# A hybrid decoder layer: the up projection as one level of Strassen's product, the gates beside the cached-key attention

## The chip, the core and the metric

The kernel is one launch on one core of a Trainium2 chip. Its engines work side by side and wait for each other by semaphores: TensorE (PE; its weight loads are listed as PEld), VectorE (DVE), ScalarE (ACT), GpSimd (POOL) and SyncE (SP), which only issues DMAs. Matmul operands stand in SBUF, matmul results in PSUM. The metric is the device time of one execution in microseconds, as a median of several runs; the profile shows one execution.

## The reference

One inference step of one decoder layer for 1024 prompt tokens and 8 sequences of 4 new tokens (32 "sample" tokens) which attend to 1024 cached tokens each, stored as 8 pages of 128. All in float32; model width 1024, FFN width 2816.

```python
proj = x @ w_in                      # q | k | v | hgrn q, f, i, g | gate_a | gate_b
oa = diff_attention(rope(q), rope(k) (+ cached pages), v)      # 4 heads, two score maps each
ob = hgrn2_scan(...)                                           # 4 heads, chunkwise
merged = sigmoid(gate_a) * (oa @ w_branch_a) + sigmoid(gate_b) * (ob @ w_branch_b)
h = layer_norm(ALPHA * x + merged @ w_out)
a, g = split(h @ w_up, 2)            # 1024 -> 2 x 2816
c = conv_b + sum(ap[:, j:j + T] * conv_w[j] for j in range(3))  # causal, over tokens
y = (gelu(c) * g) @ w_down
out = layer_norm(ALPHA * h + y)
```

Outputs are `out` for both token sets, the new keys and values, the HGRN states and the last two rows before the convolution.

## The kernel before

**Arithmetic.** A float32 product runs on TensorE as three products of a reduced type: each operand is split into a high part (ACT copies it, line 130) and a low part (DVE subtracts the high part from the value, line 131), and `mm3` (lines 225 to 227) or `mm3s` (lines 235 to 237) add high x high, low x high and high x low. A weight tile of 128x512 therefore costs one ACT cast and one DVE subtraction, from `raw`, which SP loads, into `wh` and `wl`. Activations lie transposed, features in partitions and tokens in columns.

**Stages.** (1) Input projections and the four HGRN heads. (2) Attention of the prompt: `attn(h, ...)` for four heads, eight query blocks each. A block `i` with n = 128 (i + 1) keys makes two score maps on PE (lines 634, 635; the tile `scp`, of which the pool `ps_sc` has two), masks and reduces them to row maxima on DVE (lines 638, 641, 643), takes the exponentials on ACT (line 646), combines the maps on DVE (lines 648 to 650), transposes the result on PE (line 207), copies it back on ACT (line 203), and multiplies by the values on PE (line 662). (3) Gates: `proj_gate` makes 128 columns of gate_a or gate_b for all 1056 tokens (72 matmuls of 384 and 288 columns, a tanh on ACT, line 830, and a write to the DRAM tile `gsc`, line 831). There are 16 of them, and `do_gates(n)` does the next n: 2 stand behind the HGRN heads, 3 behind `attn(0)`, 2 behind `attn(1)`, 5 behind `attn(3)` and 4 behind the first `load_o`. A scheduler lays out the order of each engine, so that a gate's matmuls stand between those of an attention that is written before it. (4) For each half of the tokens (512, and 512 with the 32 sample tokens): `merge` (gated branches, line 946 to 948; output projection; LayerNorm; `turn_`, which transposes back and splits h into the SBUF tiles `hh` and `hl`), then `ffn`.

**ffn, one half.** For each m of 22 the columns m of `a` and of `g` are two products over the eight 128-row pieces of h, with token columns in two groups (256 and 256 in the first half, one of 512 there for m of 16 and more; 256 and 288 in the second). The convolution is three DVE operations (lines 1052 to 1054), Gelu is on ACT (line 1065), the product with g on DVE (line 1071), and a split leaves u in SBUF. `down` multiplies the 22 tiles of u by `w_down`, `rows` adds ALPHA h (POOL, line 1090) and the product (DVE, line 1091), turns the result, and `ln2` normalises it (POOL, lines 1138 and 1139).

**The sample attention.** `SampleAttn` gathers cached pages with indirect DMAs that POOL issues (line 723) into a tile `pg` of two buffers; `keys(b)` transposes them on DVE (line 743) and makes the scores on PE (line 749); `values(b)` multiplies by the gathered values (line 800). In this kernel `beside` spreads the 8 calls of `keys` and the 8 of `values` over the 22 steps m of the first half's up projection. Two half passes follow each other: merge, up, down, merge, up, down.

## Time and profile before

| | |
|---|---|
| median of 3 runs | 1805.58 us (1803.87 to 1806.1) |
| the profiled execution | 1803.07 us |
| its span in the trace | 1801.3 us |
| TensorE busy | 1761.8 us, 98% |
| VectorE busy | 1035.4 us, 57% |
| ScalarE busy | 747.9 us, 42% |
| GpSimd busy | 200.0 us, 11% |

From the trace the stages lie at these times: projections and HGRN to about 315 us, attention with its gates to about 735, first merge to about 840, up of the first half with the sample attention to 1145, down to 1262, second merge to 1388, up to 1655, down to 1790. Matmuls are pipelined, so that a matmul's shown duration (280 ns for 256 columns) is longer than the distance from its start to the next start (118 ns); the distance is what a further matmul costs. For the same reason a busy share near one doesn't exclude short waits on TensorE.

### The profile page before, as it was taken

The page shows a single profiled execution, that of the slowest core. Times are in us where ns is not written, and L with a number is a line of the kernel's source. Part 1 is how long each engine was busy: PE and PEld are TensorE (multiplying, and loading weights), DVE is VectorE, ACT ScalarE, POOL GpSimd, SP SyncE. Part 2 cuts the span into 40 slices and gives each one's busy share as a digit, 9 for nine tenths or more (in the row PEclk, how much of TensorE's full clock was granted, in tenths as well). Part 3 has the DMA queues.
Part 4 walks back from the last instruction along what each step waited for, and adds up shares of the span by engine and source line. Part 5 has one row for each costly group of instructions (what it writes and reads, how often), then busy time and mean ns, then how long its engine had stood idle before and what let it go on. Part 6 is the DMA issues. An engine that isn't in the chain of part 4 may idle for free.

```text
span 1801.3 us, 33741 instructions
## 1 busy us (share of the span) xinstructions
PE 1761.8 (98%) x13652; PEld 1654.1 (92%) x13652; DVE 1035.4 (57%) x2199; ACT 747.9 (42%) x1774; POOL 200.0 (11%) x280
## 2 busy tenths in 40 slices
PE   8999999999999999998999999999899999999996
PEld 8999999999999999887989987888888999999996
DVE  5757646765656653656776454444856655554336
ACT  6466354545553544425333433223325433443223
POOL 1000010120221010003030011000500000000013
PEclk9999999999999999998999999999999999999998
DMA  6110211212221222844556466424632332323234
GB/s 214 38 61 26 83 61 42 92 47 77 84 68 39 79 75 70 270 129 142 178 176 202 143 206 196 150 88 136 219 116 83 96 91 83 94 83 89 86 91 125
DMA packets 234832, 199.37 MB, mean 111 GB/s; under 512 B 8050, under 2 KB 213106, under 8 KB 230562
## 3 DMA queue, kind: packets, MB, share of 16 engines
q1 hardware_dynamic: 218432, 140.92, 26.0%
q0 software_dynamic: 9296, 47.44, 7.4%
q10 hardware_dynamic: 6948, 8.86, 1.5%
q8 instruction: 107, 1.75, 0.4%
q14 instruction: 49, 0.40, 0.1%
HBM read 173.00 MB, written 24.19 MB: 109 GB/s over the span
## 4 chain that ended last, share of the span: by engine, by line
PE 89%; DVE 4%; DMA 3%; ACT 2%; issue 1%; POOL 1%; SPq 0%; POOLq 0%; DVEq 0%; ACTq 0%
PE mm L236 14%; PE mm L235 14%; PE mm L237 14%; PE mm L225 11%; PE mm L227 10%; PE mm L226 10%; PE tp L207 3%; PE tp L662 2%; PE sb L405 2%; PE mm L246 1%; PE scp L635 1%; PE scp L634 1%; PE mx L225 1%; PE mx L227 1%; DMA c<-gsc 1%
## 5 line engine op out<-in xcount | busy, mean ns | idle before, releaser
L131 DVE TENSOR_TENSOR wl<-raw,wh 128x512 fp32r<-128x512 f32 (+1 forms) x404 | 286.3, 714 | 368.0 <-ACT wh L130 348.1
L130 ACT CAST wh<-raw 128x512 fp32r<-128x512 f32 (+1 forms) x404 | 244.9, 612 | 489.1 <-PE mm L236 371.2
L235 PE MATMUL mm<-hh,wh 128*128 128x256 f32 (+2 forms) x1312 | 386.9, 295 | 3.3 <-ACT hh L130 2.7
L236 PE MATMUL mm<-hl,wh 128*128 128x256 f32 (+2 forms) x1312 | 387.3, 295 | 1.4 <-DVE mv L910 1.4
L237 PE MATMUL mm<-hh,wl 128*128 128x256 f32 (+2 forms) x1312 | 387.3, 296 | 0.0
L235 PEld LDWEIGHTS mm<-hh,wh 128*128 128x128 f32 x1312 | 249.2, 190 | 13.7 <-issue 4.1
L236 PEld LDWEIGHTS mm<-hl,wh 128*128 128x128 f32 x1312 | 248.7, 190 | 6.9 <-DVE hl L131 2.1
L237 PEld LDWEIGHTS mm<-hh,wl 128*128 128x128 f32 x1312 | 248.6, 190 | 5.0 <-issue 0.6
L225 PE MATMUL mm<-xh,wh 128*128 128x384 f32 (+1 forms) x560 | 186.7, 334 | 0.8 <-ACT wh L130 0.8
L226 PE MATMUL mm<-xl,wh 128*128 128x384 f32 (+1 forms) x560 | 186.9, 334 | 0.0
L227 PE MATMUL mm<-xh,wl 128*128 128x384 f32 (+1 forms) x560 | 186.0, 332 | 0.0
L225 PE MATMUL mm<-wh,xh 128*128 128x256 f32 x480 | 136.5, 285 | 0.8 <-DVE rb L578 0.8
L226 PE MATMUL mm<-wl,xh 128*128 128x256 f32 x480 | 136.3, 284 | 0.2 <-DVE wl L131 0.2
L227 PE MATMUL mm<-wh,xl 128*128 128x256 f32 x480 | 135.9, 283 | 0.0
L225 PEld LDWEIGHTS mm<-xh,wh 128*128 128x128 f32 x560 | 105.3, 188 | 4.0 <-issue 2.3
L227 PEld LDWEIGHTS mm<-xh,wl 128*128 128x128 f32 x560 | 105.4, 188 | 1.8 <-issue 1.5
L226 PEld LDWEIGHTS mm<-xl,wh 128*128 128x128 f32 x560 | 105.4, 188 | 1.3 <-issue 0.8
L225 PEld LDWEIGHTS mm<-wh,xh 128*128 128x128 f32 x480 | 90.2, 188 | 1.5 <-issue 1.0
L226 PEld LDWEIGHTS mm<-wl,xh 128*128 128x128 f32 x480 | 90.4, 188 | 0.5 <-DVE wl L131 0.4
L227 PEld LDWEIGHTS mm<-wh,xl 128*128 128x128 f32 x480 | 90.5, 189 | 0.1
L203 ACT COPY s<-tp 128x512 f32<-128x512 f32 (+3 forms) x96 | 39.5, 426 | 101.2 <-PE tp L207 42.5
L1090 POOL TENSOR_TENSOR c<-hh,hl 128x512 f32<-128x512 f32 (+2 forms) x24 | 23.3, 970 | 476.1 <-DVE u20l L131 256.8
(670 smaller groups left out, 3772.6 us busy)
## 6 DMA issues: line engine op xcount, KB each, us to landing
raw<-in_w_up_dram SPq DMA_DIRECT2D x88, 512.0 KB, 3.8
raw<-in_w_in_dram SPq DMA_DIRECT2D x44, 512.0 KB, 3.8
raw<-in_w_down_dram SPq DMA_DIRECT2D x36, 512.0 KB, 3.6
raw<-in_w_out_dram SPq DMA_DIRECT2D x16, 512.0 KB, 3.7
raw<-in_w_down_dram SPq DMA_DIRECT2D x18, 384.0 KB, 3.1
gsc<-gt ACTq DMA_DIRECT2D x32, 192.0 KB, 1.9
raw<-in_w_branch_b_dram SPq DMA_DIRECT2D x16, 256.0 KB, 5.4
raw<-in_w_branch_a_dram SPq DMA_DIRECT2D x16, 256.0 KB, 3.6
```

Source lines behind the costliest of these rows:

```text
L130: S.copy(h, src)
L131: eng.tensor_tensor(l, src, h.bitcast(F32), ALU.subtract)
L203: S.copy(out, in_)
L207: PE.transpose(out, in_, ident[:n, :n])
L225: PE.matmul(ps, lhsT=ah, rhs=bh, start=(i == 0), stop=False)
L226: PE.matmul(ps, lhsT=ah, rhs=bl, start=False, stop=False)
L227: PE.matmul(ps, lhsT=al, rhs=bh, start=False, stop=(i == n - 1))
L235: PE.matmul(ps, lhsT=ah, rhs=bh, start=(k == 0), stop=False)
L236: PE.matmul(ps, lhsT=ah, rhs=bl, start=False, stop=False)
L237: PE.matmul(ps, lhsT=al, rhs=bh, start=False, stop=(k == n - 1))
L405: PE.matmul(p[:, a * 64:a * 64 + 64], lhsT=W[:, a * 128:a * 128 + 128], rhs=rhs[:, a * nb:a * nb + nb], start=True, stop=True)
L662: PE.matmul(po[:, :128], lhsT=aT[:, j * 128:(j + 1) * 128], rhs=v_[:, j], start=(j == 0), stop=(j == i))
```

## The change

The up projection is done once for all 1056 tokens, behind both merges, and by Strassen's scheme in the form with 15 additions: h^T is cut into two halves of the features and, for the prompt, two halves of the tokens (sample tokens 0 to 15 go with the first, 16 to 31 with the second), the weights into feature halves and into a and g. Seven products of half the depth take the place of eight. `operands` and `combine` make the seven operands from h (four additions on POOL in `combine`, splits on ACT and DVE), `wcombos(m)` makes the seven from the weights (four additions on POOL, seven splits), `product` is one of the seven for 256 or 272 columns, and the loop over m puts the results together (five additions on DVE, two on POOL, two copies on ACT, for each of two column chunks).

h goes to the DRAM tile `hT` and is read back for the second merge's `combine` and in `rows`, where it was an addition on POOL. The gated rows u go through the DRAM tile `uT`: their product with g is now on POOL, and `down_half` reads them and splits them. `down` is as before, apart from m = 0 and 1 of each half, which go together. The order is now merge, merge, up, down, down. The sample attention stands behind the prompt's attention, one call of `keys` or `values` (two, at two places) beside each of 14 gates; the other two gates stand behind the first `load_o`.

```diff
     hgrn(3, *lq, g, i23[1])
-    do_gates(2)
...
     attn(0, Q[0], K[0], v[0])
-    do_gates(3)
...
     v = proj_tok(1024, 1, vsl, vs_, O["v_p"], O["v_s"])
-    do_gates(2)
...
     attn(3, Q[1], K[1], v[1])
-    do_gates(5)
...
+    sample = SampleAttn(ap, av)
+    for i in range(14):
+        do_gates(1)
+        for b in range(8 * (i % 7) // 7, 8 * (i % 7 + 1) // 7):
+            (sample.keys if i < 7 else sample.values)(b)
...
+    def combine(c, cols, b11, b12, b21, b22, t3):
+
+        def put(o, x):
+            h, l = ops[c][o]
+            split(x, h[:, :, cols], l[:, :, cols])
+
+        put(B11, b11)
+        G.tensor_tensor(t3, b22, b12, ALU.subtract)
+        G.tensor_tensor(b12, b12, b11, ALU.subtract)
+        put(B22, b22)
+        G.tensor_tensor(b22, b22, b12, ALU.subtract)
+        put(T2, b22)
+        put(B21, b21)
+        G.tensor_tensor(b21, b21, b22, ALU.subtract)
+        put(T1, b12)
+        put(T3, t3)
+        put(T4, b21)
...
-                V.tensor_tensor(ga[:, :nh], ga[:, :nh], gb_[:, :nh], ALU.add)
...
+            G.tensor_tensor(ga[:, :nh], ga[:, :nh], gb_[:, :nh], ALU.add)
...
+                G.dma_start(hT[h2 * 4:h2 * 4 + 4, :, tt:tt + tn].rearrange("k p t -> p k t"), y[:, :, :tn])
...
+                    SY.dma_start(b, hT[h2 * 4:h2 * 4 + 4, :, tt - 512:tt - 512 + tn].rearrange("k p t -> p k t"))
...
+        put(B11, a11)
+        G.tensor_tensor(s1, a21, a22, ALU.add)
+        G.tensor_tensor(s2, s1, a11, ALU.subtract)
+        put(T2, s2)
+        put(B21, a12)
+        put(T1, s1)
+        G.tensor_tensor(a11, a11, a21, ALU.subtract)
+        put(T3, a11)
+        G.tensor_tensor(a12, a12, s2, ALU.subtract)
+        put(B22, a12)
+        put(T4, a22)
...
+    def product(w, x, o, cn):
+        pturn[0] += 1
+        ps = (pst(), pmm(), ps_s.tile([128, 512], F32, tag="s", name="ps_s"), pmm())[pturn[0] % 4][:, :cn]
+        for k in range(4):
+            ah, al = (y[:, k * 128:(k + 1) * 128] for y in w[o])
+            bh, bl = (y[:, k, :cn] for y in x[o])
+            PE.matmul(ps, lhsT=ah, rhs=bh, start=(k == 0), stop=False)
+            PE.matmul(ps, lhsT=ah, rhs=bl, start=False, stop=False)
+            PE.matmul(ps, lhsT=al, rhs=bh, start=False, stop=(k == 3))
+        return ps
...
+            S.copy(m1, product(w, x, B11, cn))
+            p6 = product(w, x, T2, cn)
+            conv_in(0, m1, product(w, x, B21, cn))
+            V.tensor_tensor(m1, m1, p6, ALU.add)
+            S.copy(m5, product(w, x, T1, cn))
+            G.tensor_tensor(u4, m5, m1, ALU.add)
+            V.tensor_tensor(u3, m1, product(w, x, T3, cn), ALU.add)
+            G.tensor_tensor(gg[:, 1, o:o + cn], u3, m5, ALU.add)
+            conv_in(1, u4, product(w, x, B22, cn))
+            V.tensor_tensor(gg[:, 0, o:o + cn], u3, product(w, x, T4, cn), ALU.add)
...
+            S.activation(cc[:, :528], cc[:, :528], AF.Gelu)
+            G.tensor_tensor(cc[:, :528], cc[:, :528], gg[:, hf, :528], ALU.mult)
+            G.dma_start(uT[m, :, o:o + 512], cc[:, :512])
+            G.dma_start(uT[m, :, TP + hf * 16:TP + hf * 16 + 16], cc[:, 512:528])
...
+            raw = wide(("hs", "ae")[k % 2])
+            SY.dma_start(raw[:, :nh], uT[k, :, th:th + nh])
+            u = ut(k)
+            split(raw[:, :nh], u[:, 0, :nh], u[:, 1, :nh])
...
-            G.tensor_tensor(y, H[0][:, m, c0:c0 + cn].bitcast(F32), H[1][:, m, c0:c0 + cn].bitcast(F32), ALU.add)
+            G.dma_start(y, hT[m, :, th + c0:th + c0 + cn])
```

What the scheduler makes of it, first on PE near the end of the last attention head (the block with 384 keys: `scp` are its score maps, `tp<-ident` transposes, `tp<-s` products with the values, `mm<-xh` gates). Before:

```order
L226 MATMUL mm<-xl,wh 128x384
L634 MATMUL scp<-s_4989,s_6239 128x384
L635 MATMUL scp<-s_4991,qpad_91 128x384
L227 MATMUL mm<-xh,wl 128x384
L225 MATMUL mm<-xh,wh 128x384
L226 MATMUL mm<-xl,wh 128x384
L634 MATMUL scp<-s_4990,s_6240 128x384
L635 MATMUL scp<-s_4991,qpad_91 128x384
L207 MATMUL tp<-ident,s_7117 128x128 x2
L227 MATMUL mm<-xh,wl 128x384
L662 MATMUL tp<-s_5420,s_7125 128x128 x4
```

Now, at the same block:

```order
L219 MATMUL tp<-ident,s_6507 128x128 x5
L664 MATMUL tp<-s_4952,s_6515 128x128 x4
L636 MATMUL scp<-s_4521,s_5583 128x384
L637 MATMUL scp<-s_4523,qpad_93 128x384
L664 MATMUL tp<-s_4952,s_6515 128x128
L636 MATMUL scp<-s_4522,s_5584 128x384
L637 MATMUL scp<-s_4523,qpad_93 128x384
L219 MATMUL tp<-ident,s_6547 128x128 x4
L636 MATMUL scp<-s_4521,s_5583 128x256
L637 MATMUL scp<-s_4523,qpad_94 128x256
```

The gate matmuls that stood between the steps of a block are gone from here; they start behind the head's last score map. In the same way stand the blocks 6 and 7 of the first head and 0 to 2 of the second, the end of the second, the blocks 3 to 7 of the third and all eight of the last.

On PE at a call of `keys` (`ps_s` and `tp<-pw` are its scores, 64 matmuls in one go). Before, beside the up projection:

```order
L749 MATMUL tp<-pw,q_9082 32x256 x12
L235 MATMUL mm<-hh,wh 128x256 x2
L749 MATMUL ps_s<-pw,q_9082 32x256 x4
L236 MATMUL mm<-hl,wh 128x256
L237 MATMUL mm<-hh,wl 128x256
```

Now, beside the gates:

```order
L751 MATMUL ps_s<-pw,q_6715 32x256 x8
L751 MATMUL tp<-pw,q_6715 32x256 x8
L239 MATMUL mm<-xh,wl 128x384
L237 MATMUL mm<-xh,wh 128x384
L238 MATMUL mm<-xl,wh 128x384
```

The calls moved from the up projection to the gates: 33 to 42 gate matmuls stand between one call of `keys` and the next within a group of four.

On POOL in the up projection (`pg` are page gathers, `soc` the sample attention's result). Before, the last rows of the first half's up projection and the first of its down projection:

```order
L364 TENSOR_TENSOR mx<-mx,mhalf 128x1
L824 DMA osc<-soc 128x4x16
L723 DMA pg<-in_cache_v_dram,idx 128x2048 x6
L1090 TENSOR_TENSOR c<-hh,hl 128x512 x2
```

Now, one step m of the up projection (`S` and `raw` are the weights' additions, `hs` and `q` the results', `ae` and `c` the gated rows):

```order
L1103 TENSOR_TENSOR S<-raw 128x512
L1170 DMA uT<-ae 128x512
L1171 DMA uT<-ae 128x16
L1104 TENSOR_TENSOR S<-S,raw 128x512
L1134 MEMSET r_12680 128x2
L1169 TENSOR_TENSOR c<-c,q_12053 128x528
L1154 TENSOR_TENSOR hs<-hs 128x256
L1156 TENSOR_TENSOR q_12367<-hs 128x256
L1108 TENSOR_TENSOR raw<-raw 128x512
L1170 DMA uT<-c 128x512
L1171 DMA uT<-c 128x16
L1110 TENSOR_TENSOR raw<-raw,S 128x512
```

POOL, which had only gathers there, now has ten additions or products and four DMA issues in each of 22 steps, two of them (`L1154`, `L1156` for 272 columns) behind the rows shown.

## Rows read from the trace of the kernel before

**Rows 1.** Page, part 1: busy us, share of the span, instructions.
```profile
PE 1761.8 (98%) x13652; PEld 1654.1 (92%) x13652; DVE 1035.4 (57%) x2199; ACT 747.9 (42%) x1774; POOL 200.0 (11%) x280
```
**Rows 2.** Stretches: length, busy us (instructions) per engine, granted clock, DMA share, GB/s.
```profile
650.00:700.00 50.00, 49.53 (x354) 48.42 (x353) 26.28 (x85) 23.66 (x71) 5.70 (x11) 1.00 0.19 61
800.00:850.00 50.00, 44.79 (x290) 38.34 (x289) 30.98 (x62) 23.15 (x43) 13.75 (x25) 0.90 0.46 151
...
1200.00:1250.00 50.00, 50.00 (x224) 40.69 (x224) 21.42 (x39) 14.98 (x29) 3.89 (x3) 1.00 0.35 102
1250.00:1300.00 50.00, 43.48 (x290) 40.97 (x289) 39.25 (x59) 19.13 (x34) 23.82 (x13) 0.93 0.68 217
1350.00:1400.00 50.00, 48.03 (x291) 42.34 (x289) 33.54 (x80) 29.08 (x62) 3.15 (x5) 0.97 0.28 85
1400.00:1450.00 50.00, 50.00 (x401) 50.00 (x400) 28.27 (x56) 19.62 (x54) 0.00 (x0) 1.00 0.33 95
```
**Rows 3.** Timeline of PE, second merge: start, length, operation (24 matmuls of 256 columns).
```profile
1279.72 0.28 PE L225 MATMUL mm<-u0h,wh 128*128 128x256 f32 x1
...
1282.43 0.28 PE L227 MATMUL mm<-u7h,wl 128*128 128x256 f32 x1
```
**Rows 4.** Timeline of DVE in the last head, blocks of 1024 and 896 keys.
```profile
640.39 1.09 DVE L638 TENSOR_REDUCE nmx<-scp 128x1 f32<-128x896 f32 x1 [0.46 <-PE scp L635]
641.52 0.36 DVE L641 CUSTOM_DVE_ANT_0 scp<-scp,cst,nmx 128x128 f32<-128x128 f32 x1
...
641.97 0.17 DVE L643 TENSOR_SCALAR nmx<-nmx 128x2 f32<-128x2 f32 x1
...
645.66 1.28 DVE L650 SCALAR_TENSOR_TENSOR s<-s,cc,s 128x1024 f32<-128x1024 f32 x1
```
**Rows 5.** Timeline of all engines: products with the values, exponentials of 256 and 128 keys.
```profile
690.06 1.38 PE L662 MATMUL tp<-s,s 128*128 128x128 f32 x10 [0.24 <-ACT s L203]
...
690.88 0.48 ACT L646 ACTIVATE s<-scp,nmx 128x256 f32<-128x256 f32 x1 [0.70 <-DVE nmx L643]
...
693.24 0.37 ACT L646 ACTIVATE s<-scp,nmx 128x128 f32<-128x128 f32 x1 [0.40 <-DVE nmx L643]
```
**Rows 6.** Groups by form, ACT: exponential of 1024 keys; busy us, mean ns, idle before.
```profile
L646 ACT ACTIVATE s<-scp,nmx 128x1024 f32<-128x1024 f32 x8 | 8.9, 1120 | 0.0
```
**Rows 7.** DMA issues: gathers of cached keys, median us from issue to landing.
```profile
pg<-in_cache_k_dram,idx POOLq DMA_INDIRECT x16, 7.1
```
**Rows 8.** Timeline of DVE: the transposes for one call of `keys`, two page tiles.
```profile
863.28 4.62 DVE L743 STREAM_TRANSPOSE pw<-pg 128x1024 f32<-128x1024 f32 x4
```
**Rows 9.** What PE waited for, over the whole span: us, times, longest.
```profile
PE mm L225 <- DVE c L946: 7.5, 3, 5.6
PE tp L207 <- DVE c L1091: 5.8, 1, 5.8
```
**Rows 10.** Groups by form, DVE: busy us, mean ns, idle before.
```profile
L131 DVE TENSOR_TENSOR wl<-raw,wh 128x512 fp32r<-128x512 f32 x386 | 279.0, 728 | 356.1 <-ACT wh L130 336.2 <-PE mm L237 16.3
L1054 DVE SCALAR_TENSOR_TENSOR c<-ae,pt,c 128x512 f32<-128x512 f32 x44 | 32.9, 748 | 0.7
...
L1071 DVE TENSOR_TENSOR c<-c,mm 128x256 f32<-128x256 f32 x54 | 21.4, 419 | 45.5 <-PE mm L237 42.8 <-ACT ae L1036 1.3 <-issue 0.7
```
**Rows 11.** Groups by form, POOL: busy us, mean ns, idle before.
```profile
L1090 POOL TENSOR_TENSOR c<-hh,hl 128x512 f32<-128x512 f32 x8 | 10.4, 1298 | 94.2 <-PE tp L207 83.8 <-DVE u21l L131 10.3
...
L1090 POOL TENSOR_TENSOR c<-hh,hl 128x256 f32<-128x256 f32 x8 | 6.4, 805 | 340.2 <-DVE u20l L131 256.8 <-PE tp L207 83.4
...
L684 POOL DMA_DIRECT2D osc<-s x8 | 4.5, 563 | 16.0 <-DVE s L683 14.8 <-DVE cc L648 0.6 <-DVE cc L649 0.3
```
**Rows 12.** Timeline of POOL, start of the second merge.
```profile
1271.91 7.63 POOL L1138 TENSOR_TENSOR z<-z,z 128x1024 f32<-128x1024 f32 x3 [2.47 <-DMA c<-gsc]
```
**Rows 13.** Timeline of DVE, the same stretch.
```profile
1277.20 0.41 DVE L946 SCALAR_TENSOR_TENSOR c<-c,mm 128x256 f32<-128x256 f32 x1
1277.53 2.56 DVE L131 TENSOR_TENSOR wl<-raw,wh 128x512 fp32r<-128x512 f32 x1
```

More of the change, by code (lines that the diff above doesn't have):

```diff
@@ L53, in hybrid_step @@
     osc = dp.tile([8, 128, T], F32, name="osc")
+    hT = dp.tile([8, 128, T], F32, name="hT")
+    uT = dp.tile([NM, 128, T], F32, name="uT")
     ident = cp.tile([128, 128], F32, name="ident")
@@ new lines, in hybrid_step, with operands @@
+    CHUNK = (256, 272)
+    ops = []
+    def operands():
+        c0 = []
+        for o in range(7):
+            pair = []
+            for i in range(2):
+                home = {(T4, 0): 0, (T4, 1): 1, (T3, 1): 4}.get((o, i))
+                pair.append(h0.tile([128, 4, 256], F32R, name=f"h0_{o}{i}") if home is None else rt(home, (4, 256), F32R))
+            c0.append(pair)
+        ops.append(c0)
+        ops.append([[qt(o * 2 + i).rearrange("p a t -> p (a t)").rearrange("p (k t) -> p k t", k=4) for i in range(2)] for o in range(7)])
@@ new lines, in merge, with wcombos, put @@
+                late = [(r, t, tt, tn)]
+            for x in late:
+                turn_(*x)
+    merge(Ot, 0)
+    Ot = load_o(*HALVES[1][:2])
+    merge(Ot, 1)
+    w_up, w_dn = I["w_up"][0], I["w_down"][0]
+    def wcombos(m):
+        ra, rg = wraw(), wraw()
+        SY.dma_start(ra.rearrange("p (k c) -> p k c", k=8), wview(w_up, m * 128, 128))
+        SY.dma_start(rg.rearrange("p (k c) -> p k c", k=8), wview(w_up, DFF + m * 128, 128))
+        s1, s2 = (wx[0].tile([128, 512], F32, tag="S", name="S", bufs=2) for _ in range(2))
+        a11, a12, a21, a22 = ra[:, :512], ra[:, 512:], rg[:, :512], rg[:, 512:]
+        out = {}
+        def put(o, x):
+            out[o] = whl()
+            split(x, *out[o])
+        put(B11, a11)
[9 more added lines that the diff above has]
+        put(T4, a22)
+        return out
@@ L1156, in ffn @@
             conv_out()
[L1157 to L1196 removed]
+        else:
+            ln2(0, 4)
+    down_half(0)
+    down_half(1)
 def _consts():
```

396 lines of the change are left out of this document (191 added, 205 removed).

## The prediction

> **What bounds the kernel now.** First the busy times: TensorE is busy 1761.8 of 1801.3 us, GpSimd 200 us [rows 1]. Then the table of stretches: in the up projection (1400 to 1450) and the down projection (1200 to 1250) PE is busy for all 50 us at a granted clock of 1.00, and near the end of the attention (650 to 700) for 49.5 [rows 2]. Only the seams between the half passes fall behind: 44.8, 43.5 and 48.0 busy at clocks of 0.90, 0.93 and 0.97 [rows 2]. So the time is PE's work plus a little, almost everywhere. A change can win by taking matmuls away, and loses wherever it opens holes in PE's order that earlier work filled. PE's busy time hides short holes, so I cost holes from the work and the chain, not from busy shares.
>
> **Price of a matmul.** 256 columns: from 1279.72 to 1282.43 are 23 distances, 0.118 us each [rows 3]. In 1400 to 1450 matmuls of 256 and 288 columns alternate, 401 in 50 us, 0.1247 each [rows 2]; 272 is their mean width, so I use 0.1247 for it. 512: 224 in 50 us, 0.223 [rows 2]. 384 and 288 lie on the same line, some 0.17 and 0.13.
>
> **The change part by part.**
>
> *Up products, −60.* Before: in the first half 16 steps of 96 matmuls of 256 columns (2 outputs, 8 pieces, 3 products, 2 groups) and 6 of 48 of 512: 16 x 96 x 0.118 + 6 x 48 x 0.223 = 181 + 64 = 245; second half 22 x 96 x 0.1247 = 263. Together 508. After: 22 steps of 7 products of 12 matmuls in two chunks, 22 x 84 x (0.118 + 0.1247) = 448.5, or 20.4 us a step. That all lies on the path. Merges, down, gates, projections keep their matmuls.
>
> *Attention without gates, +58.* In the order, 18 blocks (6 and 7 of the first head, 0 to 2 of the second, 3 to 7 of the third, all of the fourth) and the end of the second head lose the gate matmuls that stood between their steps. The gates are not cheaper elsewhere, so each hole is lost. `ps_sc` holds one block's two score maps, so a block's steps can overlap little with the next one's. For 1024 keys the path of a block is: score matmuls of the first map, 4 x 0.223 = 0.9; on DVE the reduction and mask of each map, 640.39 to 641.97 is 1.6, twice 3.2, then 0.17 [rows 4]; the first exponential 1.12 [rows 6]; with five hand-overs of some 0.15 (an estimate from the 0.1 to 0.2 between neighbouring rows) 6.2. If the combination of the maps, 1.28 [rows 4] and 0.4 of small steps, gets between, 7.9. PE's own work in it: 8 x 0.223 for scores, 8 transposes and 8 value products at about 0.12 (1.38 for 10 overlapping ones [rows 5]), 3.7. Hole: 2.5 to 4.2. For 256 keys the end of the last head shows the pace without filler: 690.88 to 693.24, 2.4 us [rows 5], for 4 x 0.118 + 4 x 0.12 = 0.95 of work: 1.4. The 18 blocks have 87 x 128 keys, 619 on average; between 1.4 and 3.35 (the middle of 2.5 and 4.2) that is 2.3 each, 42 us. The end of the second head, where one head's last block, normalisation and transposes follow each other, I put at 10 (about 1.5 of the long chains), and 6 for a clock that falls in such holes, as it did to 0.90 at a seam [rows 2]. Bounds: if only DVE's own work sets the pace, a 1024-key block costs 3.2 + 0.17 + 0.4 + 1.28 = 5.0 against 3.7, a hole of 1.3, 23 for 18 blocks and nothing else; at worst 18 x 3.2 + 10 + 18 = 85, with half clock for a good part. I take 58, nearer to the chain, because the two blocks that are seen without filler go at the chain's pace.
>
> [...]
>
> *Sample attention beside gates, +12.* The up projection hid it completely. A call of `keys` needs two page tiles and there are two buffers, so a buffer's cycle is 7.1 us for the gather [rows 7], 2.3 for half of the 4.62 of transposes [rows 8], about 1 for the issue: 10.4 a call. PE has 37 gate matmuls between calls, 37 x 0.158 = 5.9, and 64 score matmuls, whose price with four side by side no row gives: 0 at the least, 64 x 0.118 = 7.5 at the most, so the hole is 0 to 4.5. I take 2, for 6 calls that follow another directly. Bounds 0 and 27. Value calls use the page directly and I let them hide.
>
> *Seams, +13.* Before: the three stretches of seams lose 5.2 + 6.5 + 2.0 of busy time and (0.10 + 0.07 + 0.03) x 50 = 10 by the clock [rows 2], 24 together; the largest waits are 7.5 for the merge's gated rows and 5.8 for the end of down [rows 9]. After: between the merges nothing, since the second merge's products cover the first one's turn. Between second merge and up all operands must be made: 33 splits on DVE, 24 additions on POOL at 0.8 to 1.3 [rows 10, 11], most beside the output projection's tail; 7 if the last tile alone counts, 28 if the two engines exclude each other; 17. Up to down: last convolution (three steps of 0.75 [rows 10]), Gelu, product on POOL 1.3, write and read back at 2 to 3 us each, split: 9. Down to down 3, since u's buffers are refilled as they come free. Clock 8. Sum 37, less 24: 13; bounds −5 and +30.
>
> *Up's other engines, +6.* Per step of 20.4 us, POOL: four additions of 512 at 1.30, four of 256 or 272 at 0.81, two products at 1.30, four issues at 0.56 [rows 11]: 13.3. DVE: seven splits at 0.73, four convolution steps at 0.75 and two at 0.54, ten additions at 0.42 to 0.45, small ones 1: 15.8 [rows 10]. Each fits. But they hinder each other: while POOL ran additions of 1024 columns, 2.5 us each (three in 7.63 [rows 12]), a DVE split took 2.56 instead of 0.7, yet a step with a PSUM operand 0.41 as ever [rows 13]. A DVE step with two SBUF inputs that meets a POOL step waits until it ends. With eleven such DVE steps and some half of the time a POOL step running, half a POOL step each: 11 x 0.55 x 0.6 = 3.6, DVE 19.4 of 20.4. That still fits, and eight PSUM tiles give a few us of slack. I take 6 over the whole phase; bounds 0 and 66 (below).
>
> [...]
>
> The splits of u move to down (44 tiles of about 0.7 on DVE, beside 118 us of matmuls a half): hidden. Reading h and u back is under 15 MB: hidden but for the seams.
>
> **Rivals.** (a) *Faster*: DVE alone paces the attention. Scores of the next block start as soon as the first exponential is done, so the small steps overlap and the holes are 23, not 58. Then −60 + 23 + 12 + 13 + 6 = −6: 1800, and 1788 if the pages hide too. Against it: 2.4 us for 0.95 of work in the seen block [rows 5]. The sum turns faster than before when the holes stay under 26 (−60 + 31 + 26 < −3.6). (b) *Much slower*: POOL and DVE pace the up projection: if most of the eleven DVE steps wait for a whole POOL step (11 x 0.55 to 0.8), DVE needs 23 to 24 a step, 22 x 3 = 66 more: 1900. It decides when the waits of DVE exceed 4.6 a step. For it: the split of 2.56 [rows 13]; against it: there POOL ran without a pause. (c) *The win is not there*: 272 columns could cost more than the mean of 256 and 288, or accumulating only four pieces per tile could leave PE waiting for PSUM; at 0.01 a matmul 18 us, 1852.
>
> **How the numbers follow.** The profiled run took 1803.07, its span 1801.3; the median is 1805.58, 2.5 above that run, and I keep that distance. −60 + 58 + 12 + 13 + 6 = +29: 1834. Chances: forecast (1812 to 1860) 0.50, (a) 0.27, (b) 0.13, (c) 0.05, an even end between 0.05. What a measurement can tell from no change is about 0.2%, 3.6 us. Faster 0.27, same 0.05, slower 0.68. The range leaves out the far ends of (a) and (b): 1780 to 1888.
>
> **What would show it.** In the changed kernel's stretches: about 20.4 us of PE per step m in the up phase, at clock 1.00 (right), or PE waiting there for DVE's or POOL's operands (b). In the attention, periods of 6 to 8 us for blocks of 1024 keys and PE waits for ACT's copies and exponentials (right), or about 5 (a). Beside the gates, PE waiting for `pw` for about 2 us a call. Wrong would be an up phase not 60 us shorter, or an attention that loses under 26 us.

## The result, and the profile after

| | before | after |
|---|---|---|
| median | 1804.72 us (1803.4 to 1806.1) | 1908.74 us (1900.04 to 1912.89) |
| ratio of the runs, 95% interval | | 1.057 [1.053, 1.061] |
| profiled execution, its span | 1803.07, 1801.3 us | 1900.04, 1897.9 us |

Slower, as forecast, but by 104 us where the forecast was 29, and outside its range (1780 to 1888). The runs of the changed kernel spread over 13 us and the profiled one is the lowest; so below the totals are medians, and the places are read from traces, whose spans differ by 96.6 us. One run of one kernel below (v4, at 2943 us) lies far from its four others and is left out.

The page of the changed kernel, part 1, answers [rows 1]:

```profile
PE 1756.1 (93%) x13412; PEld 1635.9 (86%) x13412; DVE 1219.7 (64%) x2425; ACT 719.2 (38%) x1683; POOL 582.8 (31%) x664
```

PE has 240 matmuls fewer and is busy for 6 us less, yet the span is 97 us longer: PE now stands still, or runs at half clock, which lengthens its busy time (at 1120 its matmuls of 256 columns follow each other every 0.213 us, at full clock every 0.118 [rows 3]). The table of stretches of the changed kernel, with the columns of [rows 2], shows where. In this order: the end of HGRN, the attention (two rows), the seam between the merges, the seam from the second merge to up, up, the seam from up to down.

```profile
300.00:350.00 50.00, 45.02 (x369) 40.70 (x369) 29.66 (x93) 25.51 (x93) 7.63 (x11) 0.93 0.19 64
550.00:600.00 50.00, 40.02 (x230) 34.21 (x228) 33.62 (x102) 26.67 (x79) 5.59 (x16) 0.93 0.08 25
600.00:650.00 50.00, 39.92 (x245) 36.33 (x246) 28.00 (x100) 24.15 (x73) 7.81 (x13) 0.86 0.11 37
950.00:1000.00 50.00, 36.45 (x181) 30.72 (x180) 24.41 (x56) 19.74 (x35) 8.85 (x13) 0.80 0.55 177
1100.00:1150.00 50.00, 25.39 (x115) 23.36 (x116) 45.34 (x55) 23.78 (x49) 32.95 (x31) 0.59 0.25 69
1200.00:1250.00 50.00, 50.00 (x412) 50.00 (x411) 46.71 (x76) 14.95 (x38) 35.03 (x35) 1.00 0.30 91
1600.00:1650.00 50.00, 47.77 (x193) 37.06 (x192) 25.29 (x45) 21.46 (x39) 1.63 (x3) 0.89 0.70 218
```

Of these only up is as full as the attention and the up and down projections of before were [rows 2]. It makes 412 matmuls in 50 us: 22 x 168 matmuls take 449 us. Between 1100 and 1150 PE is busy for 25 us, at a mean clock of 0.59, while DVE has 45 us of work and POOL 33: this seam alone costs some 36 us.

What PE waited for over the whole span of the changed kernel (us, times, longest), the largest entries; they answer [rows 9]:

```profile
PE tp L219 <- ACT r L1075: 18.5, 4, 8.0
PE tp L219 <- DVE s L652: 12.4, 9, 2.7
PE scp L636 <- ACT s L648: 11.2, 11, 4.6
PE mm L237 <- DMA raw<-in_w_branch_a_dram: 8.3, 1, 8.3
PE mm L1213 <- ACT x L131: 7.9, 2, 5.6
PE tp L219 <- DVE s L682: 7.8, 2, 4.2
PE tp L219 <- DVE c L1223: 7.2, 2, 5.6
PE mm L237 <- ACT q L131: 5.4, 2, 5.0
PE mm L1121 <- ACT h L131: 4.3, 1, 4.3
```

The second, the third and the sixth (the end of a head) are the attention; the others are seams (a normalised row to turn, a weight tile of the first merge, operands of down, the last rows of down, operands of the second merge and of up).

**Stage by stage.** I took each stage's length in both traces less its matmuls at full clock (the prices of the prediction; 0.17 for 384 columns). What is left is lost. HGRN: 60 before, 75 after. Attention with what stands beside it: 8 and 68. Then the seams and what lies between them, after: 13 for the wait ahead of the first merge and that merge (before 6), 22 for the seam between the merges and the second merge (18 for the second merge before, its seam with down included), 36 from the second merge into up, where before there was nothing, 13 in the rest of up (4 before), 12 from up to down, 7 and 28 for the two halves of down (4 and 18). The records of the clock show half clock for 167 us in the changed kernel, in 18 stretches, and for 36 in the kernel before.

### The profile page after: what moved, and what is told of

Same layout as the page of the kernel before. It is cut to its first block, busy times and chain, and to the rows that moved or that the text cites. A ratio compares the mean times of both kernels' runs of the same rounds, so it can differ in the third digit from the quotient of the medians.

```text
span 1897.9 us, 34200 instructions
## 1 busy us (share of the span) xinstructions
PE 1756.1 (93%) x13412; PEld 1635.9 (86%) x13412; DVE 1219.7 (64%) x2425; ACT 719.2 (38%) x1683; POOL 582.8 (31%) x664
## 5 line engine op out<-in xcount | busy, mean ns | idle before, releaser
L132 DVE TENSOR_TENSOR wl<-raw,wh 128x512 fp32r<-128x512 f32 x370 | 275.0, 750 | 241.4 <-ACT wh L131 217.9
L131 ACT CAST wh<-raw 128x512 fp32r<-128x512 f32 x370 | 220.3, 609 | 342.2 <-PE mm L1214 107.8
L237 PE MATMUL mm<-xh,wh 128*128 128x384 f32 (+1 forms) x576 | 191.7, 333 | 1.2 <-ACT wh L131 0.8
L239 PE MATMUL mm<-xh,wl 128*128 128x384 f32 (+1 forms) x576 | 191.3, 332 | 0.0
L1215 PE MATMUL mm<-q,wl 128*128 128x512 f32 (+2 forms) x384 | 124.9, 326 | 2.6 <-DVE wl L132 2.6
L1213 PE MATMUL mm<-q,wh 128*128 128x512 f32 (+2 forms) x384 | 124.7, 325 | 0.0
L1214 PE MATMUL mm<-q,wh 128*128 128x512 f32 (+2 forms) x384 | 124.5, 324 | 0.0
L1222 POOL DMA_DIRECT2D c<-hT x24 | 13.1, 547 | 221.9 <-PE tp L219 92.9
L1215 PEld LDWEIGHTS mm<-q,wl 128*128 128x128 f32 x384 | 72.3, 188 | 8.1 <-DVE wl L132 2.8
L1121 PE MATMUL mm<-h,wh 128*128 128x256 f32 x264 | 74.9, 284 | 4.3 <-ACT h L131 4.3
L1214 PEld LDWEIGHTS mm<-q,wh 128*128 128x128 f32 x384 | 72.4, 189 | 5.9 <-DVE q L132 0.4
```

The costliest lines, as they stand in the source:

```text
L131: S.copy(h, src)
L132: eng.tensor_tensor(l, src, h.bitcast(F32), ALU.subtract)
L237: PE.matmul(ps, lhsT=ah, rhs=bh, start=(i == 0), stop=False)
L239: PE.matmul(ps, lhsT=al, rhs=bh, start=False, stop=(i == n - 1))
L1121: PE.matmul(ps, lhsT=ah, rhs=bh, start=(k == 0), stop=False)
L1213: PE.matmul(ps, lhsT=ah, rhs=bh, start=(k == 0), stop=False)
```

## Experiments

Where two kernels are compared by medians, the 13 us over which the changed kernel's runs spread stand behind each difference. Of the traces I give what the stage itself lost. Two traces differ ahead of any edit too: the first score map comes at 355.4 in the changed kernel, at 353.0 in e5 and at 361.0 in e9, whose code up to there is the same. So a difference of some 8 us between two spans need not come from an edit.

### What the gates, the sample attention and the rest cost: e1, e2, e4, e8

Three kernels without the sample attention. In e1 the changed kernel has only its 14 gates there; e2 is e1 with 12 gates back where the kernel before had them; e4 is the kernel before without it.

```diff
-    sample = SampleAttn(ap, av)
-    for i in range(14):
-        do_gates(1)
-        for b in ...: (sample.keys if i < 7 else sample.values)(b)
+    do_gates(14)                # e1; in e2 do_gates(2)
...
+    do_gates(2)                 # e2: behind hgrn(3); 3 behind attn(0), 2 ahead of
+                                # attn(2), 5 behind attn(3)
```

> The changed kernel without the sample attention over the cached pages (its gathers, transposes, scores and values are left out, so the sample tokens' attention output is zero); all 16 gates stay where they are. Theory (PE holes: the loss sits in the attention and HGRN heads without gates, about 75 us, and in the seams, about 60 us): the sample attention costs only its own PE work, some 30, and a hole of about 12, so 1860 us (1850 to 1875). Rival (the sample attention beside the gates is the main loss, because its gathers don't keep up): 80 us or more, below 1825.

> As e1_no_sample (the sample attention over the pages is left out), and 12 of the 16 gates go back to the places of the kernel before: 2 behind the HGRN heads, 3 behind the first attention head, 2 behind the second, 5 behind the fourth. Same PE work as e1. Theory: the holes of the attention and of the last HGRN head are filled again, 65 to 80 us less than e1, about 1785. Rival (the attention is slower for another reason, such as the order of its own steps): within 15 us of e1.

> The kernel before without the sample attention over the cached pages (left out; its output columns are zero). Up of the first half with it took about 311 us in the profile, its own matmuls 245. Theory: 50 to 60 us of PE work of the sample attention fall away and little else, since the up projection hid its gathers: 1745 to 1757 us. With the 73 us that the changed kernel lost without it, the change then made it dearer by 15 to 25 us. Rival (before hid it wholly, PE work included, in holes): above 1780.

Measured: e1 1835.61 us, ratio to before 1.018 [1.012, 1.024]; e2 1761.48, 0.977 [0.972, 0.983]; e4 1746.35, 0.969 [0.966, 0.972]. e2 and e4 came out as expected; e1 fell between its theory (1850 to 1875) and its rival (below 1825). From e1 to e2, the gates' place alone, the time falls by 74; by spans 76. Between 550 and 600 e2 has the density of the kernel before again (that kernel's row first):

```profile
550.00:600.00 50.00, 50.00 (x384) 49.46 (x384) 37.35 (x127) 20.84 (x68) 7.04 (x15) 1.00 0.22 71
```

```profile
550.00:600.00 50.00, 50.00 (x385) 49.46 (x384) 37.36 (x127) 20.26 (x67) 7.04 (x15) 1.00 0.22 69
```

The sample attention costs 73 in the changed kernel (1908.74 less 1835.61) and 56 in the kernel before, so moving it costs 17 by medians; by spans, which rest on the changed kernel's fastest run, 62 against 57, so 5. What e2 and e4 differ in is then the product with 7 terms and everything around it: +15. Up gives 60 back, so the seams and up's other engines cost 75. These three differences add up to the whole by construction (by medians but for some 2 us, by which the kernel before differs from one set of runs to another); what they show is the size of each.

e8 moves two gates only, back behind HGRN, from behind the first `load_o`.

```diff
     hgrn(3, *lq, g, i23[1])
+    do_gates(2)
...
     Ot = load_o(*HALVES[0][:2])
-    do_gates(2)
```

> The changed kernel with the two gates that stand behind the first load of the attention's output moved back behind the last HGRN head, where the kernel before had them. My prediction priced their removal there at nothing. If HGRN loses them as the stage table reads (74.9 us lost against 60.1, and 13.7 of half clock): 10 to 15 us less at HGRN, but the load before the first merge then loses the cover of 11.4 us of gate matmuls; so 1897 to 1908 in all, with the lost time of the HGRN stage down to 60 to 63 in the trace. If HGRN's holes are its own: the stage stays at 75 and the time rises by up to 8, to 1917.

Measured: 1892.80 us, 1.051 [1.048, 1.054], 16 less, 4 below the expected range; by spans 6 less. (The two gates have 2 x 72 matmuls, 23 us; the 11.4 in the expectation is one of them.) The first score map comes 9 us later than in the changed kernel (364.3 against 355.4), with 23 us of gates ahead of it: HGRN gets 14 back. Its stretch in the kernel before, and then in e8:

```profile
300.00:350.00 50.00, 50.00 (x391) 46.91 (x390) 26.58 (x82) 22.03 (x79) 7.61 (x11) 1.00 0.18 63
```

```profile
300.00:350.00 50.00, 50.00 (x390) 46.91 (x389) 25.52 (x79) 21.98 (x78) 7.62 (x11) 1.00 0.19 63
...
850.00:900.00 50.00, 33.05 (x238) 26.19 (x237) 21.96 (x36) 13.51 (x25) 8.20 (x7) 0.76 0.63 202
```

The last row is the price: without its two gates the first `load_o` leaves PE idle for 17 of 50 us, where the changed kernel has 10.

### The seams: e5, e7, e3, e9

e5 moves the four additions of `combine` from POOL to DVE and nothing else.

```diff
-        G.tensor_tensor(t3, b22, b12, ALU.subtract)
-        G.tensor_tensor(b12, b12, b11, ALU.subtract)
+        V.tensor_tensor(t3, b22, b12, ALU.subtract)
+        V.tensor_tensor(b12, b12, b11, ALU.subtract)
...
```

and the same for the other two.

> The changed kernel with one edit: the four additions of combine, which make the operands between the second merge and the up projection, on DVE instead of POOL. DVE gets 16 additions of 512 columns more, some 11 us. Theory (POOL and DVE hold each other up there, so that DVE's splits of 0.7 us take 1.7): the stretch from the last merge matmul to the up projection's pace falls from 49 by 8 to 15 us, 1890 to 1900 in all. Rival (DVE's own work is what counts there): 0 to 11 us more.

Measured: 1883.37 us, 1.044 [1.041, 1.047]: 25 less by medians, 16.5 by spans, of which 16 lie between the first and the last product of up (495.6 us in the changed kernel, 479.7 here). More than expected, though DVE was the fuller engine and got more work. The timelines say why. DVE's splits in the seam of the changed kernel (start, length, operation; some of those over 1.6 us, and one of 0.69):

```profile
1109.90 1.62 DVE L132 TENSOR_TENSOR r<-c,r 128x512 fp32r<-128x512 f32 x1
1111.45 5.86 DVE L132 TENSOR_TENSOR h<-hs,h 128x512 fp32r<-128x512 f32 x1
1117.38 0.69 DVE L132 TENSOR_TENSOR q<-c,q 128x512 fp32r<-128x512 f32 x1
1117.99 1.75 DVE L132 TENSOR_TENSOR r<-hs,h 128x512 fp32r<-128x512 f32 x1
...
1122.46 2.07 DVE L132 TENSOR_TENSOR h<-hs,h 128x512 fp32r<-128x512 f32 x1
```

and POOL's additions beside the second and third of them:

```profile
1111.74 1.29 POOL L976 TENSOR_TENSOR hs<-hs 128x512 f32<-128x512 f32 x1
...
1113.02 1.26 POOL L1104 TENSOR_TENSOR S<-S,raw 128x512 f32<-128x512 f32 x1
1114.24 1.26 POOL L977 TENSOR_TENSOR hs<-hs,ae 128x512 f32<-128x512 f32 x1
...
1115.50 1.25 POOL L1108 TENSOR_TENSOR raw<-raw 128x512 f32<-128x512 f32 x1
1117.44 1.75 POOL L979 TENSOR_TENSOR hs<-hs 128x512 f32<-128x512 f32 x1 [0.69 <-DVE h L132]
```

A split of a form that takes 0.69 us alone, as the one at 1117.38 does, is on the engine from 1111.45 to 1117.31, while four additions of POOL follow each other (two of `combine`, L976 and L977, and two of the weights') and the last ends at 1116.75; 0.56 later it is done. Behind it, the addition at 1117.44 meets the split at 1117.38 and takes 1.75 instead of 1.26, and the split of 1117.99 meets that addition and takes 1.75. Between 1090 and 1146 seventeen of DVE's splits take over 1.2 us each in the changed kernel, together some 24 us more than alone, and two in e5. PE meanwhile waits for what these queues have still to make, as its timeline shows (in brackets the idle time before, and what ended it):

```profile
1107.25 1.11 PE L219 MATMUL tp<-ident,r 128*128 128x128 f32 x4 [7.99 <-ACT r L1075]
...
1111.63 1.11 PE L219 MATMUL tp<-ident,r 128*128 128x128 f32 x4 [2.42 <-ACT r L1075]
...
1117.92 0.58 PE L1121 MATMUL mm<-h,wh 128*128 128x256 f32 x1 [4.32 <-ACT h L131]
1119.79 0.58 PE L1122 MATMUL mm<-r,wh 128*128 128x256 f32 x1 [1.29 <-DVE r L132]
```

The wait of 7.99 is the second merge's last rows: statistics and splits on DVE, and the `rstd` that POOL had queued among the additions (L366 at 1100.21 and 1107.16). In the stretch from 1100 to 1150 e5 is much fuller:

```profile
1100.00:1150.00 50.00, 37.57 (x266) 36.39 (x267) 47.09 (x89) 27.08 (x54) 24.34 (x26) 0.80 0.32 96
```

It has 266 matmuls there, the changed kernel 115. How much of the gain is the two engines no longer holding each other up, and how much the shorter queue on POOL, in which the `rstd` stands, e5 does not separate.

e7 sets back the counters that deal weight tiles over two pools, so that other tiles of the first merge lie on the space that the gates' operands hold until the last gate.

```diff
     wx[0] = w2s.enter_context(tc.tile_pool(name="wx", bufs=1))
+    wturn[:] = [0, 3]
```

> One edit to the changed kernel: the counters that deal the weight tiles over the pools are set back where the pool for the merge is opened, so that other weight tiles of the first merge fall on the space that the gates' operands hold until the last gate. No arithmetic changes. If the 8.3 us for which TensorE waits for a weight tile at 880 are the turn's doing: 4 to 9 us less than the changed kernel, 1899 to 1904. If the wait is set by the last gate's end whatever tile is first, or if the merge then waits for the gated rows instead: within 2 us of 1908.

Measured: 1886.15 us, 1.046 [1.044, 1.048]: 23 less by medians, 12 by spans, and 13 below the expected range. From the last gate to the first product of up it takes 213.2 us instead of 224.0, so 11 lie there. The wait to be removed, in PE's timeline of the changed kernel:

```profile
879.84 0.76 PE L237 MATMUL mm<-q,wh 128*128 128x512 f32 x1 [8.30 <-DMA raw<-in_w_branch_a_dram]
```

is gone, and the stretch from 850 to 900, which had 40.27 us of PE work, now has

```profile
850.00:900.00 50.00, 49.47 (x304) 42.72 (x303) 24.24 (x41) 17.53 (x34) 7.21 (x6) 1.00 0.68 213
```

So that wait was a matter of where a tile stands, and it costs 11 with the clock that fell behind it. Where the other half of the medians' 23 comes from can't be told: the slower runs of the changed kernel have no trace.

e3 has e5's edit, and with it other buffers for the loads of the attention's output and of u, a DRAM tile of its own for the sample attention's heads, and the additions of `ln2` partly on DVE.

```diff
+    oss = dp.tile([4, 128, T - TP], F32, name="oss")
...
-            raw = wide(("hs", "ae")[k % 2])
+            raw = wide(("c" if nh > 512 else "hs", "ae")[k % 2])
...
-            raw = wide(("hs", "ae")[k % 2])
+            raw = us.tile([128, 544], F32, tag="ur", name="ur", bufs=2)
...
-                np_ = D if i == 4 or not half else 512 if i == 1 else 0
+                np_ = D if i == 4 else 512 if half and i == 1 else 0
```

> The changed kernel with five edits at its seams only: combine's additions on DVE instead of POOL, the sample heads' output in a DRAM tile of its own, the second load_o through other buffers, u read back through two buffers of its own, and the first half's LayerNorm finished on DVE instead of POOL. Gates and sample attention untouched. Theory (the seams lose about 45 us more than forecast, through loads queued behind buffers and through POOL and DVE excluding each other): 20 to 45 us less, 1860 to 1885. Rival (the seams are the chain of LayerNorm and operands itself, which these edits leave alone): within 10 us of the changed kernel, 1895 to 1912.

Measured: 1880.89 us, 1.043 [1.034, 1.053]: 28 less than the changed kernel, but only 2.5 less than e5 by medians, 8 by spans. That is within the expected range, but by medians nearly all of it goes with the four additions. The loads do help the seam between the merges (206 us from the last gate to up, with 224 in the changed kernel and in e5); behind up e3 gives much of that back (321.7 us from up's last product to the end of the trace, with 309.4 in e5 and 306.8 in the changed kernel).

e9 puts 300 transposes of the unit matrix ahead of the first five products of up, to keep the clock from falling.

```diff
         ps = (pst(), pmm(), ps_s.tile(...), pmm())[pturn[0] % 4][:, :cn]
+        if pturn[0] <= 5:
+            for _ in range(60):
+                transpose(ps[:, :128], ident)
```

> The changed kernel with 300 transposes of the unit matrix into the PSUM tiles of the first five products of the up projection, 60 ahead of each; their results are overwritten by the products. They add work to TensorE where it waits for the operands. If the half clock behind the second merge (24 + 10 + 7 us in the trace) costs time by itself: the clock stays at 1.00 for most of 1100 to 1160 and the time falls by 5 to 15, to 1894 to 1904. If the operands set that seam's end and the clock only falls in time that is lost anyway: the same within 3, 1905 to 1912, or longer by what the transposes take.

Measured: 1909.88 us, 1.059 [1.057, 1.062], the same as the changed kernel. The half clock of that seam fell from 41 us to 7, as the stretch of 50 us behind 1112 shows (compare 1100 to 1150 above):

```profile
1112.00:1162.00 50.00, 42.27 (x349) 41.86 (x348) 36.13 (x42) 17.48 (x37) 27.31 (x25) 0.93 0.21 62
```

Here PE is busy for 42 us and nothing is gained; by traces, from the last matmul of the second merge to the last product of up, e9 takes 503 us where the changed kernel took 496. So raising the clock does not bring this seam's end forward; PE still waits for the operands. The test is not clean: the transposes take PE time themselves, and some of them waited for a PSUM tile that `turn_` had not yet read (5.89 us at 1128). It shows that the half clock is no cost of its own there beyond what the filler cost, not that it is free everywhere.

### What is left when all of it is undone in part: v1 to v9, e6

These join the edits above with gates given back: how many of the 16 stand again in the attention's order, and what else changed from one to the next. All sample calls stand ahead of the rest of the gates, with four buffers for the pages. Each row of the table below carries the edits of the rows above it, except v4, which is v2 with one edit; its `ln2` edit is one of e3's, which v2 had taken out.

> The edits of e3_seams, and seven gates back in the HGRN and attention stages (2, 2, 1, 2), nine left beside the sample attention, whose page tile gets four buffers and whose transposed tile two. Theory: holes of attention and HGRN 45 to 60 less, seams 20 to 45 less, the sample attention somewhat less covered (+10): 1800 to 1850. Rival (with fewer gates the sample attention comes out uncovered by as much as the attention gains): no better than e3_seams, 1860 to 1885.

> v1_combined with these differences: eight gates back (2, 2, 1, 3) and eight beside the sample attention; the first merge's first two weight tiles in buffers that don't wait for the projections' space; the pools h0 and rp in the other order, so that the buffers for u don't lie where the last convolution works; u read back through seven buffers in turn instead of two; LayerNorm of the first half on POOL as in the changed kernel. Theory: 9 us at the first merge, 8 at up to down, 10 in the down projections, some half clock with each: 1805 to 1825. Rival (the lost time moves to the next seam): above 1835.

> v2_combined with nine gates back (2, 3, 1, 3) and seven beside the sample attention. Theory: the attention gains what the sample attention loses, within 8 us of v2_combined.

> v2_combined with the LayerNorm of the first half's output finished on DVE instead of POOL. Theory (POOL's additions of 1024 columns hold up DVE's splits at the start of the second down projection): 5 to 10 us less than v2_combined. Rival (DVE has no room there): 5 to 10 us more.

> v4_combined with eight gates back and eight beside the sample attention; in addition the operand tiles q0 to q7 don't lie on the sample attention's space, so that the first merge can begin beside the sample's values, and the second merge's transposed tiles leave PSUM through ACT alone. Theory: the wait before the first merge (10 us and a half clock) goes, and 3 us at the seam to up: 1795 to 1808. Rival (the first merge needs its other tiles too soon): within 5 us of v4_combined, 1817.

> v5_values_beside_merge with nine gates back in the attention (2, 3, 1, 3) and seven beside the sample attention. Theory: since the first merge now covers part of the values, another gate is worth more in the attention: 2 to 6 us less than v5_values_beside_merge. Rival: the sample attention comes out uncovered, 3 to 8 us more.

> v6_nine_gates_back with 90 transposes of a constant tile, 0.11 us each, whose result nobody reads, behind the second merge, where PE waits for operands and the granted clock falls to 0.5 for some 20 us. Theory (part of a seam's price is the half clock after the idle time): the clock stays at 1.00 there or falls for less, and 3 to 8 us less in all. Rival (only the wait itself counts): no difference, or up to 8 us more, by what the filler itself delays.

> The kernel with nine gates back and the dummy transposes, with one edit: the tiles of the sample attention's result (sum over heads, its square, the result that is written) stand in the buffers that the merges use, not in the pool of the pages. Before it the first merge waited 8.5 us for a weight tile and its operands, released by the write of that result, since their space was the pages'. If that wait is the result's tiles: 5 to 9 us less than 1810, 1801 to 1805, level with the kernel before. If the pages themselves hold the space as long: 1808 to 1812.

> The same with ten of the sixteen gates back in the attention's order (one more beside the second head), and six beside the sample attention's values. One gate more there gives 4 to 6 us by the price of the other gates (74 us for twelve), and takes the cover of 11 us of gate matmuls from the values, of which the output projection may give back some: 1797 to 1806 if the values are then covered by the merge's matmuls, 1804 to 1812 if the merge waits for them.

> The same with eleven gates back (one more behind the last head) and five beside the values. If the attention's end still has holes to fill: 3 to 5 us less than with ten, 1793 to 1802. If the values then lack cover: 3 to 8 more, 1801 to 1812.

| kernel | gates back | further edit | median us | ratio to before |
|---|---|---|---|---|
| v1 | 7 | e3's edits | 1846.72 | 1.024 [1.019, 1.030] |
| v2 | 8 | e7's; u loads over more buffers; two pools in the other order | 1820.31 | 1.010 [1.007, 1.013] |
| v3 | 9 | none | 1825.47 | 1.013 [1.010, 1.016] |
| v4 | 8 | `ln2` partly on DVE again | 1816.5 | 1.007 [1.005, 1.009] |
| v5 | 8 | the values beside the gates behind `load_o`; turned tiles of the second merge through ACT alone | 1814.06 | 1.006 [1.003, 1.009] |
| v6 | 9 | none | 1813.27 | 1.005 [1.002, 1.008] |
| e6 | 9 | 90 transposes behind the second merge | 1810.38 | 1.004 [1.002, 1.006] |
| v7 | 9 | the sample's result tiles in other buffers | 1811.42 | 1.004 [1.003, 1.005] |
| v8 | 10 | none | 1817.60 | 1.008 [1.006, 1.009] |
| v9 | 11 | none | 1818.37 | 1.008 [1.007, 1.010] |

None beats the kernel before. v1 to v3 came out as expected. v4 gained some 4 us where 5 to 10 were expected; v5 and v7 came out as their rivals had it; v6 gained 1 where 2 to 6 were expected, and v8 and v9 lie above both of their ranges. The edits to one of them are as short as

```diff
-            dst = self.av.tile([128, 4, 512], F32, tag="pg", name="pg", bufs=2)
+            dst = self.av.tile([128, 4, 512], F32, tag="pg", name="pg", bufs=4)
...
+    do_gates(2)                 # v4: behind hgrn(3), 2 behind attn(0), 1 ahead of attn(2), 3 behind attn(3)
...
+    for b in range(8):
+        sample.keys(b)
+    aps.close()
+    for b in range(8):
+        sample.values(b)
+    do_gates(6)
```

Three readings. From v6 to e6 the difference of 3 us lies within the spread, and the half clock behind the second merge only fell from 14 us to 10, so e6 says little on what it costs. v7 was to remove a wait ahead of the first merge, 8.5 us in v6 and 7.2 in e6, and most of it stayed: 5.9, with another releaser. In v6 and then in v7 (each from its own list of PE's waits):

```profile
PE mm L238 <- DMA raw<-in_w_branch_a_dram: 8.5, 1, 8.5
```

```profile
PE mm L238 <- ACT wh L132: 6.6, 2, 5.9
```

The space was not held by the result tiles alone; what holds it longest stays open. And v8 and v9 show the limit: each gate given to the attention is one less beside the sample attention's values. In v9, with eleven back, PE waits for pages again:

```profile
PE tp L803 <- DMA pg<-in_cache_v_dram,idx: 7.5, 4, 2.9
...
PE mm L238 <- issue: 4.9, 1, 4.9
```

There are 16 gates, some 180 us of PE work, and three takers: attention, HGRN and sample attention. In the kernel before up covered the third.

## Why the prediction was wrong

**Up, −60: right.** 22 steps of 20.4 us were forecast, 449 us; the trace has 412 matmuls in 50 us at clock 1.00, 0.1214 each, and the mean of the two prices of the forecast (0.118 and 0.1247) is that. Rival (c) is out.

**Up's other engines, +6: near, though for a narrow margin.** The rest of up lost 9 more than before (13 less 4). DVE is busy for 46.7 and POOL for 35.0 of 50 us in up. A step of 20.4 us then has 19.1 us of DVE; forecast were 19.4, but the terms listed for DVE add up to 14.5 and not 15.8, so by its own terms the forecast was 18.1. Rival (b) is out. The groups by form of the changed kernel between 1150 and 1590 show the hindrance that the prediction took from [rows 13] (busy us, mean ns, idle before):

```profile
L132 DVE TENSOR_TENSOR wl<-raw,wh 128x512 fp32r<-128x512 f32 x109 | 86.1, 791 | 3.2 <-ACT wh L131 3.2
L132 DVE TENSOR_TENSOR wl<-S,wh 128x512 fp32r<-128x512 f32 x40 | 51.6, 1289 | 0.1
```

**Attention, +58: right as a sum in the attention, and it left HGRN out.** The attention lost 59.5 more than before (67.7 less 8.2). The blocks went at the pace of the long chain, as the exponentials of ACT show; two blocks of 1024 keys and their neighbour are 7.7 and 7.2 us apart, against a forecast of 6 to 8:

```profile
581.52 1.01 ACT L648 ACTIVATE s<-scp,nmx 128x896 f32<-128x896 f32 x1 [1.02 <-DVE nmx L645]
...
589.23 1.11 ACT L648 ACTIVATE s<-scp,nmx 128x1024 f32<-128x1024 f32 x1 [0.79 <-DVE nmx L645]
...
596.42 1.13 ACT L648 ACTIVATE s<-scp,nmx 128x1024 f32<-128x1024 f32 x1
```

Rival (a) is out. The parts were less right than the sum. By the distances between matmuls (an estimate), 14 to 16 of the 68 us are matmuls at half clock, where the forecast had 6 for the clock; the holes then cost some 45 more than before, where it had 52. And the step priced 18 blocks and a head's end, and gave the two gates behind HGRN no price: the trace lost 15 there, and e8 gave 14 of it back. So the whole change of gates cost 74 to 76 (e1 to e2), not 58.

**Sample attention, +12: within what can be told.** It cost 5 by spans and 17 by medians.

**Seams, +13: the step that failed.** They and up's engines cost 75 (e2 against e4, with up at −60), and 19 were forecast. By pieces, with the forecast beside them:
- "Between the merges nothing": 15.8 lost at 974 to 990. The second merge's products did not cover the first one's turn: its own operands came late, since SP's loads of them stood behind loads of x (L1016) that waited for buffers. PE's timeline there:

```profile
974.55 0.66 PE L219 MATMUL tp<-ident,r 128*128 128x128 f32 x4 [2.18 <-ACT r L1075]
981.60 1.11 PE L219 MATMUL tp<-ident,r 128*128 128x128 f32 x4 [5.96 <-ACT r L1075]
988.61 0.82 PE L237 MATMUL mm<-q,wh 128*128 128x256 f32 x2 [5.04 <-ACT q L131]
```

- Merge to up, 17, with a bound of 28 if the two engines exclude each other: 36. I had seen a split wait in [rows 13] (2.56 us instead of 0.7) and used that for up, but put 17 here, nearer to no hindrance; e5, which takes 16 of it away, says that the bound was nearer, and the bound left out that POOL would also hold back DVE for several additions in a row (5.86 us for one split, over four of them), and the `rstd` of the last rows behind them.
- Ahead of the first merge the sum had no term: 8.3 of waiting, 11 with what followed (e7). The diff does not show it; which space a pool's tile falls on decides it.
- Up to down, 9: 11.6, of which 5.64 is one wait for u:

```profile
1597.04 0.76 PE L1213 MATMUL mm<-x,wh 128*128 128x512 f32 x1 [5.64 <-ACT x L131]
```

- Clock, 8: the changed kernel has 131 us more of half clock. By the distances between matmuls, work in such stretches took some 35 to 43 us longer than at full clock over the whole kernel (an estimate), 8 to 9 of it in the seam to up. How much of that would have gone into waits anyway the runs leave open; e9, which raised the clock, gained nothing.
- The second half of down lost 10.6 more than before; the waits over 1.5 us account for 4 of it. The rest stays open.

**Range.** Its upper end, 1888, was set without the far end of rival (b) for up (1900). Nothing in it stood for several seams at once near their bounds, though the prediction gave seams a bound of +30. The attention with HGRN's gates, the sample and the seams at that bound would have given −60 + 74 + 17 + 30 + 6, or 67: 1873. The measured 1909 needed the unpriced waits as well.

What DVE and POOL did to each other can be read in both directions. DVE behind POOL: the split of [rows 13] ended 0.55 us after the third addition of [rows 12], and the split of 5.86 above ended 0.56 after the last of four. POOL behind DVE, for which the prediction had no row: the addition at 1117.44 took 1.75 instead of 1.26 beside a split that had begun at 1117.38.

## What to carry to other kernels

Before a stage is joined or moved, list what filled whose holes: here 16 gates covered three latency-bound stages, up covered a fourth, and a saving of 60 us in matmuls was smaller than the 74 of cover it took away. At a seam where an engine's operands are made, try additions and splits on one engine rather than on two: here, where one split of 0.69 us took 5.86 beside POOL's additions, more work on the busy engine was 16 to 25 us faster. And a wait that no line of the diff shows can come from where a pool's tile lies (8.3 us here, gone in e7); look, for every first load behind a freed pool, at who frees it last.

## What the chip showed that I had not expected

- A DVE operation with two SBUF inputs did not get in between POOL's additions when they followed each other directly: one split of 0.69 us took 5.86, over four of them. One wait per POOL operation was too low a price here.
- POOL's addition of 272 columns in up (L1154) took 1.855 us on average, and the same of 256 took 0.739:

```profile
L1154 POOL TENSOR_TENSOR hs<-hs 128x272 f32<-128x272 f32 x22 | 40.8, 1855 | 31.5 <-DVE hs L1152 27.7 <-ACT hs L1153 3.8
...
L1154 POOL TENSOR_TENSOR hs<-hs 128x256 f32<-128x256 f32 x21 | 15.5, 739 | 0.0
```

  The 16 columns do not explain 1.1 us: in the same stretch POOL's product of 528 columns (L1169, `c`) took 1.330 on average and its addition of 512 (L1108) 1.295. The addition of 272 is released by a DVE addition and so starts where DVE is at work. In one step of up, two DVE steps with two tile inputs lie across it one after the other, and it ends 0.64 behind the second:

```profile
1175.27 0.74 DVE L1162 SCALAR_TENSOR_TENSOR ae<-r,pt,ae 128x512 f32<-128x512 f32 x1
1175.93 0.68 DVE L132 TENSOR_TENSOR wl<-raw,wh 128x512 fp32r<-128x512 f32 x1
```

```profile
1175.30 1.95 POOL L1154 TENSOR_TENSOR hs<-hs 128x272 f32<-128x272 f32 x1 [0.32 <-DVE hs L1152]
```

- The prediction let only DVE steps with two tile inputs wait. The first convolution step has one, and a column of factors; where an addition of POOL (L1110) is already running when it starts, as for `ae` in 21 of 22 steps, it takes 1.28 to 1.30; the one of `ae` that meets none takes 0.55, and those of `c`, which meet none, 0.53 to 0.55. So POOL holds up such a step too:

```profile
L1161 DVE TENSOR_SCALAR ae<-r,pt 128x512 f32<-128x512 f32 x22 | 27.6, 1254 | 0.0
...
L1161 DVE TENSOR_SCALAR c<-r,pt 128x512 f32<-128x512 f32 x21 | 11.3, 537 | 0.0
```

- In the attention without gates the granted clock fell to 0.5 in stretches of 3 to 10 us, 44 us in all, behind holes of PE of 2.7 to 4.6 us, or behind several short ones (1.27, 0.73, 1.24 and 0.79 ahead of the stretch at 583). PE's work that falls in such a stretch takes nearly twice as long: matmuls of 256 columns follow each other every 0.213 us between 1120.17 and 1124.65, at a clock of 0.5, where 0.118 is the distance at 1.00 [rows 3]. So such holes can cost more than their length.
- Filling a seam with dummy matmuls raised its clock from 0.59 to 0.93 and bought nothing; PE still waited for the operands, though the filler took PE time itself.
